# Two-layer diffusion trunk on one core: context and latent tokens packed to 1152 columns, with a padded tile for the convolutions alone

## The chip, the core and the metric

The kernel runs as one program on one core of a Trainium2 chip. The core has five engines with queues of their own: TensorE (PE; its weight loads are shown as PEld), VectorE (DVE), ScalarE (ACT), GpSimd (POOL) and SyncE (SP). Here SP issues the loads and POOL the stores. The metric is the time of one execution on the device in microseconds; lower is better. Before the change it is 2097.41 us, the median of three runs (2095.89 to 2098.44).

## What is computed

Two layers run over 128 context tokens and 1024 latent tokens with the same weights, D = 1024. Layer 0 has a Mamba-2 part (SSD) and a Hyena part (a long convolution by FFT); layer 1 is neighbourhood attention. Cut to what the change touches:

```
for l in range(2):
    h = rms_norm(x, norm_w[l]) * (1 + scale) + shift          # context and latent have their own scale, shift, gate
    if l == 0:
        z_a, xbc, dt_raw, u_b, g_b = split(h @ w_in)
        xbc = silu(depthwise_conv(xbc, conv_a_w, conv_a_b))   # 3 taps along the tokens, zeros beyond both ends
        y_a = rms_norm(ssd(xbc, dt_raw) * silu(z_a), norm_a_w)
        x0, x1, v = split(depthwise_conv(u_b, conv_b_w, conv_b_b))
        y_b = x0 * fft_long_conv(v * x1, k, hy_bias) * silu(g_b)
        out = concat([y_a, y_b]) @ w_out
    else:
        q, k, v, g = split(h @ w_in)
        out = (attention(q, k, v) * silu(g)) @ w_out
    x = x + gate * out
y = rms_norm(x, final_norm_w)
```

Context and latent are separate sequences: each convolution sees zeros before the first and behind the last token of each. The final SSD states and the context's keys and values are outputs too.

## The kernel before

Activations lie channel by channel: a tile holds 128 channels on the partitions and all tokens in its columns. Context and latent tokens share a tile. The context stands in columns 0 to 127, the latent in 130 to 1153 (`OFF` = 130); columns 128, 129 and 1154 to 1157 hold zeros, so the tile has `T` = 1158 columns, three blocks of `NB` = 386. The zeros are what a three-tap convolution needs between the two sequences and behind the last; every other step carries them along.

**Projections.** `proj` multiplies 128 output channels by all tokens. For each of three blocks it goes over the eight (in the output projection four) tiles of 128 input channels with three matmuls each, the high part of the weights by the high part of the activation (L157), high by low (L158) and low by high (L159), into one PSUM buffer of the tag `pj`, which has three. Then `evac` empties the buffer. `proj_k` with `proj_step` (L184 to L186) does the same with the loop over input channels outside, for the first chunks of a stage, whose input is still being made; `dt_proj` (L615, L616) is a small projection for dt. The values (L1167 to L1169) use 256 columns and the last projection (L1366 to L1368) 512, outside of this blocking.

**The norm.** `rstd_rep` makes 1/rms of each token, repeated over the partitions: the sum of squares comes from PE in `bg`, DVE scales it to `ms` (L326), POOL raises it to a power, `rs` (L328), DVE spreads it on a diagonal (`diag`, L334), PE multiplies that by ones (L337), and ACT copies it out (L341 to L345), with the context and the latent apart in the first third. DVE clears the pads (L330, L331). `make_h` then makes the tiles `hh` and `hl` (high and low part of h) on DVE and ACT (L359 to L365), and POOL casts the pads into each of the 16 tiles (L368, L369).

**Convolutions.** `conv_chunk` runs 36 times: for 12 chunks of xbc and 24 of u_b. It empties each block with two ACT instructions, `raw` (L586) and `acc` (L587: scaled by the middle tap, with the bias), and then adds the two outer taps on DVE in two passes over 1157 columns (L596, L598). `raw` has one buffer, `acc` three. Where the result goes to token order, `to_tokens` transposes it in slices of 128, which `tk` finds.

**Other users of the layout.** `silu2` makes z and the gates block by block (L849 on ACT, L850 on DVE). `x0g_main` loads the FFT's result `ycd`, multiplies it by the convolved x0 (L873) and by the gate with a factor 0.5 (L876). `y_tile` loads the SSD's y in two pieces around the pads and clears the pads. The output projection adds x in its part 2 (L1100, two pieces) and clears pads of x1 in part 0 (L1103, POOL). The FFT's result `yc` (tag X, one buffer) and attention's `og` have their pads cleared by DVE.

**Order.** Each engine runs its instructions in the order in which the Python code issues them. The generators of background work (SSD, FFT, the filter) are advanced by `tick` between the blocks of a projection, so that their small matmuls (`bg`) lie between the large ones; how many steps a tick takes is set by hand. POOL's queue mixes the stores with the few instructions that POOL computes, in the same order of issue, and a store waits in the queue until its tile is written.

Of the kernel before, what the change touches and what calls it, by code (L numbers as in the profile page):

```python
# [9 lines left out]
AF = mybir.ActivationFunctionType  # L10
# [6 lines left out]
OFF = 130  # L17
T = 1158
NB = 386
NCH = 9  # L20
# [16 lines left out]
def tk(c):  # L37
    return 0 if c == 0 else OFF + 128 * (c - 1)

# [5 lines left out]
class Net:  # L45
# [267 lines left out]
    def rstd_rep(self, acc, pool, ncnt, tag="tt", fill=(), p=None):  # L313

        fill = list(fill)
        nc = self.nc
        if p is None:  # L320
# [5 lines left out]
        nc.vector.tensor_scalar(out=ms, in0=p[:, :NCH], scalar1=1.0 / ncnt, scalar2=EPS, op0=ALU.mult, op1=ALU.add)  # L326
        r = self.t(pool, [128, NCH], "rs", bufs=1)
        nc.gpsimd.tensor_tensor(out=r, in0=ms, in1=self.mh, op=ALU.pow)  # L328
        rep = self.t(pool, [128, T], tag, bufs=1)
        nc.vector.memset(rep[:, 128:OFF], 0.0)  # L330
        nc.vector.memset(rep[:, OFF + 1024:T], 0.0)  # L331
        for g in range(3):
            dg = self.t(pool, [128, 3, 128], "diag", bufs=self.nd)
            nc.vector.tensor_tensor(out=dg, in0=bc(self.ident.unsqueeze(1), [128, 3, 128]),  # L334
                                    in1=bc(r[:, 3 * g:3 * g + 3].unsqueeze(2), [128, 3, 128]), op=ALU.mult)
            q = self.ps()
            nc.tensor.matmul(q[:, :384], self.ones, dg.rearrange("p a b -> p (a b)"), start=True, stop=True)  # L337
            if fill:
                fill[g - 3]()
            if g == 0:  # L340
                nc.scalar.copy(rep[:, 0:128], q[:, 0:128])  # L341
# [11 lines left out]
    def make_h(self, l, k, x, rep, slot):  # L353
# [13 lines left out]
        for sl in (slice(128, OFF), slice(OFF + 1024, T)):  # L367
            nc.gpsimd.tensor_copy(hi[:, sl], rep[:, sl])  # L368
            nc.gpsimd.tensor_copy(lo[:, sl], rep[:, sl])  # L369
# [208 lines left out]
    def conv_chunk(self, cols, pool, ps=None):  # L578

        nc = self.nc  # L580
        raw = self.t(pool, [128, T], "raw")
        acc = self.t(pool, [128, T], "acc", bufs=3)
        self.raw = raw

        def evac(b, sl, p):
            nc.scalar.copy(raw[:, sl], p)  # L586
            nc.scalar.activation(acc[:, sl], p, AF.Identity, bias=cols[:, 3:4], scale=cols[:, 1:2])  # L587
# [8 lines left out]
        V.scalar_tensor_tensor(out=acc[:, 1:T], in0=raw[:, 0:T - 1], scalar=cols[:, 0:1], in1=acc[:, 1:T],  # L596
                               op0=ALU.mult, op1=ALU.add)
        V.scalar_tensor_tensor(out=acc[:, 0:T - 1], in0=raw[:, 1:T], scalar=cols[:, 2:3], in1=acc[:, 0:T - 1],  # L598
# [72 lines left out]
    def to_tokens(self, src, dst, pool, tag, bufs):  # L671

        nc = self.nc
        o = self.t(pool, [128, T], tag, bufs=bufs)[:, 0:NCH * 128].rearrange("p (c n) -> p c n", n=128)

        def run():
            for c0 in range(0, NCH, 4):
                n = min(4, NCH - c0)
                p = self.ps()
                for j in range(n):  # L680
                    nc.tensor.transpose(p[:, j * 128:(j + 1) * 128], src[:, tk(c0 + j):tk(c0 + j) + 128], self.ident)
                nc.scalar.copy(o[:, c0:c0 + n], p[:, :n * 128].rearrange("p (a c) -> p a c", c=128))
# [4 lines left out]
    def xbc(self, pool):  # L687
# [7 lines left out]
        for j in range(12):  # L695
# [25 lines left out]
    def fft(self, g, u, pool):  # L721
# [63 lines left out]
        V.memset(yc[:, 128:OFF], 0.0)  # L785
        V.memset(yc[:, OFF + 1024:T], 0.0)
# [77 lines left out]
    def x0g_main(self, pool, second):  # L864
        nc = self.nc
        cv = self.pv[:, PV["cvb"]:PV["cvb"] + 96].rearrange("p (m j) -> p m j", j=4)
        for g in range(8):
# [3 lines left out]
            yc = self.t(pool, [128, T], "acc", bufs=3)  # L871
            self.dma(yc, self.ycd[g])
            nc.vector.tensor_tensor(out=yc, in0=yc, in1=x0, op=ALU.mult)  # L873
# [196 lines left out]
    def out0(self, part, ys, x1, pool, tail=None, mid=None, order=range(4)):  # L1070
# [24 lines left out]
        for m in range(8):  # L1095
            if part == 2:
                xr = self.t(pool, [128, T], "yr")
                self.dma(xr, self.i["xT"][:, m])
                for st, s in self.STR:
                    nc.vector.tensor_tensor(out=x1[m][:, st], in0=x1[m][:, st], in1=xr[:, st], op=ALU.add)  # L1100
            if part == 0:
                for sl in (slice(128, OFF), slice(OFF + 1024, T)):
                    nc.gpsimd.memset(x1[m][:, sl], 0.0)  # L1103
# [149 lines left out]
    def attn(self, j, qt, kt, vc, pool):  # L1253
# [17 lines left out]
        V.memset(og[:, 128:OFF], 0.0)  # L1271
        V.memset(og[:, OFF + 1024:T], 0.0)
# [583 lines left out]
```

## Time and profile before

| | us |
|---|---|
| median of 3 runs | 2097.41 |
| profiled execution | 2094.29 |
| its span | 2092.5 |
| PE busy | 2033.5 |
| DVE busy | 1316.1 |
| ACT busy | 908.5 |
| POOL busy | 122.8 |

The profile shows one execution. Its groups of instructions give line, engine, operation, tile written <- tiles read, shape and count, then busy time and the mean duration of one in ns, then the idle time of the engine just ahead of them with what ended most of it. Neighbouring matmuls overlap, so the mean duration of one is longer than their distance from each other. Of a window, the profile tells for each engine the busy time in it and the number of instructions. By the trace, the stages follow each other as the start and h (to about 60 us), xbc (to 210), z (to 500), Hyena's x1 and v with the FFT (to 850), x0 and its gate (to 1085), the output projection (to 1330), the norm ahead of layer 1 (to 1375), q, k, values, gates and attention (to 1980), and the end.

### The profile page before, as it was taken

The page shows a single profiled execution, that of the slowest core. Times are in us where ns is not written, and L with a number is a line of the kernel's source. Part 1 is how long each engine was busy: PE and PEld are TensorE (multiplying, and loading weights), DVE is VectorE, ACT ScalarE, POOL GpSimd, SP SyncE. Part 2 cuts the span into 40 slices and gives each one's busy share as a digit, 9 for nine tenths or more (in the row PEclk, how much of TensorE's full clock was granted, in tenths as well). Part 3 has the DMA queues.
Part 4 walks back from the last instruction along what each step waited for, and adds up shares of the span by engine and source line. Part 5 has one row for each costly group of instructions (what it writes and reads, how often), then busy time and mean ns, then how long its engine had stood idle before and what let it go on. Part 6 is the DMA issues. An engine that isn't in the chain of part 4 may idle for free.

```text
span 2092.5 us, 33870 instructions
## 1 busy us (share of the span) xinstructions
PE 2033.5 (97%) x13088; PEld 1836.8 (88%) x13088; DVE 1316.1 (63%) x2774; ACT 908.5 (43%) x2031; POOL 122.8 (6%) x241
## 2 busy tenths in 40 slices
PE   5999999999999999999999999999999999999998
PEld 3999997889999999888888899898888888888877
DVE  6888744145778787998889774644444344453464
ACT  4766643153333322644466512535445454443231
POOL 1110001110000000000000000200000000000000
PEclk9999999999999999999999999999999999999999
DMA  9142358554212113433353441332332223333462
GB/s 347 37 164 77 106 185 289 188 188 156 85 65 79 57 58 101 167 115 134 111 166 107 139 156 50 112 86 82 97 110 85 83 73 96 110 116 121 118 223 81
DMA packets 115417, 257.36 MB, mean 123 GB/s; under 512 B 27159, under 2 KB 63639, under 8 KB 112791
## 3 DMA queue, kind: packets, MB, share of 16 engines
q1 hardware_dynamic: 99880, 192.01, 28.9%
q0 software_dynamic: 15376, 63.18, 8.3%
q8 instruction: 104, 1.70, 0.3%
q14 instruction: 57, 0.47, 0.1%
HBM read 187.25 MB, written 67.89 MB: 122 GB/s over the span
## 4 chain that ended last, share of the span: by engine, by line
PE 51%; issue 5%; DVE 4%; DMA 2%; ACT 1%; POOL 0%; POOLq 0%; SPq 0%; DVEq 0%; ACTq 0%
PE pj L157 9%; PE pj L158 8%; PE pj L159 8%; PE bg L1329 3%; PE bg L1341 3%; PE bg L1312 3%; PE pj L1167 2%; PE pj L1168 2%; PE pj L1169 2%; PE pj L1366 1%; PE pj L1367 1%; PE pj L1368 1%; PE bg L993 1%; PE bg L1027 1%; PE bg L1006 1%
## 5 line engine op out<-in xcount | busy, mean ns | idle before, releaser
L157 PE MATMUL pj<-hh,whi 128*128 128x386 f32 x1728 | 605.0, 350 | 2.0 <-DVE gs L850 1.2
L158 PE MATMUL pj<-hl,whi 128*128 128x386 f32 x1728 | 592.2, 343 | 0.0
L159 PE MATMUL pj<-hh,wlo 128*128 128x386 f32 x1728 | 590.5, 342 | 0.0
L157 PEld LDWEIGHTS pj<-hh,whi 128*128 128x128 f32 x1728 | 327.4, 189 | 22.8 <-issue 17.9
L158 PEld LDWEIGHTS pj<-hl,whi 128*128 128x128 f32 x1728 | 326.9, 189 | 7.4 <-issue 6.3
L159 PEld LDWEIGHTS pj<-hh,wlo 128*128 128x128 f32 x1728 | 327.5, 190 | 5.4 <-issue 4.5
L130 DVE TENSOR_TENSOR wlo<-wraw,whi 128x1024 fp32r<-128x1024 f32 x108 | 131.8, 1221 | 161.7 <-ACT whi L129 154.3
L129 ACT CAST whi<-wraw 128x1024 fp32r<-128x1024 f32 x108 | 113.2, 1049 | 261.5 <-PE pj L158 227.2
L1245 DVE CUSTOM_DVE_ANT_0 sz<-bg,Tb 128x512 f32<-128x512 f32 x128 | 83.5, 687 | 128.6 <-PE bg L1312 128.0
L586 ACT COPY raw<-pj 128x386 f32<-128x386 f32 x105 | 50.4, 482 | 165.2 <-PE pj L159 76.0
L1247 ACT ACTIVATE sz<-sz,mx 128x512 f32<-128x512 f32 x128 | 91.5, 716 | 55.1 <-DVE mx L1245 54.9
L158 PE MATMUL pj<-ylo,whi 128*128 128x386 f32 x324 | 111.7, 345 | 0.0
L157 PE MATMUL pj<-yhi,whi 128*128 128x386 f32 x324 | 110.0, 340 | 0.2 <-DVE x L1084 0.2
L159 PE MATMUL pj<-yhi,wlo 128*128 128x386 f32 x324 | 109.7, 339 | 0.0
L1343 ACT COPY Pt<-bg 128x512 f32<-128x512 f32 (+1 forms) x144 | 71.9, 549 | 32.2 <-PE bg L1341 28.3
L1167 PE MATMUL pj<-whi,hh 128*128 128x256 f32 x288 | 83.5, 291 | 0.0
L1168 PE MATMUL pj<-wlo,hh 128*128 128x256 f32 x288 | 81.9, 285 | 0.0
L1169 PE MATMUL pj<-whi,hl 128*128 128x256 f32 x288 | 81.3, 283 | 0.0
L1341 PE MATMUL bg<-csq,sz 128*128 128x128 f32 x528 | 73.8, 280 | 0.0
L911 ACT ACTIVATE xw<-xt,wd 128x64 f32<-128x64 f32 x256 | 64.6, 336 | 8.2 <-PE bg L918 8.1
L1341 PEld LDWEIGHTS bg<-csq,sz 128*128 128x128 f32 x528 | 56.6, 140 | 13.0 <-issue 12.8
L1084 DVE SCALAR_TENSOR_TENSOR x<-pj,mod,x 128x128 f32<-128x128 f32 (+1 forms) x96 | 46.4, 512 | 29.1 <-PE pj L159 24.8
(427 smaller groups left out, 4041.2 us busy)
## 6 DMA issues: line engine op xcount, KB each, us to landing
wraw<-in_we SPq DMA_DIRECT2D x52, 512.0 KB, 3.7
wa<-in_wada SPq DMA_DIRECT2D x32, 512.0 KB, 6.9
wraw<-in_wo SPq DMA_DIRECT2D x24, 512.0 KB, 3.8
Tb<-Cd SPq DMA_DIRECT2D x256, 48.0 KB, 2.0
Hd<-H POOLq DMA_DIRECT2D x8, 1280.0 KB, 5.7
H<-Hd SPq DMA_DIRECT2D x8, 1280.0 KB, 6.7
xt<-xtd SPq DMA_DIRECT2D x17, 512.0 KB, 4.3
wraw<-in_woe SPq DMA_DIRECT2D x16, 512.0 KB, 3.6
```

Of the source, the lines that this page charges most:

```text
L129: self.nc.scalar.copy(hi, r)
L130: self.nc.vector.tensor_tensor(out=lo, in0=r, in1=hi.bitcast(F32), op=ALU.subtract)
L157: nc.tensor.matmul(p[:, :NB], wh, xh[k][:, sl], start=(k == 0), stop=False)
L158: nc.tensor.matmul(p[:, :NB], wh, xl[k][:, sl], start=False, stop=False)
L159: nc.tensor.matmul(p[:, :NB], wl, xh[k][:, sl], start=False, stop=(k == nk - 1))
L1167: nc.tensor.matmul(p[:, :256], self.hh[k][:, ts], hi[:, q:q + 256], start=(k == 0), stop=False)
L1168: nc.tensor.matmul(p[:, :256], self.hh[k][:, ts], lo[:, q:q + 256], start=False, stop=False)
L1169: nc.tensor.matmul(p[:, :256], self.hl[k][:, ts], hi[:, q:q + 256], start=False, stop=(k == 7))
L1245: V.tensor_tensor_reduce(out=z[:, :n], in0=s, in1=tb, scale=-1.0, scalar=3.0e38, op0=ALU.add, op1=ALU.min, accum_out=m1)
L1247: nc.scalar.activation(z[:, :n], z[:, :n], AF.Exp, bias=m1, scale=-1.0, accum_out=sm)
L1341: nc.tensor.transpose(pt[:, b * 128:(b + 1) * 128], p[:, b * 128:(b + 1) * 128], self.ident)
L1343: nc.scalar.copy(t[:, :nb * 128], pt[:, :nb * 128])
```

## The change

The latent tokens now follow the context's directly: `OFF` = 128, `T` = 1152, `NB` = 384. Only `conv_chunk` keeps a padded layout, with `PO` = 130 as the latent's first column and `TP` = 1154 columns. In it the first block (128 context and 256 latent columns) is emptied in two pieces, on each side of columns 128 and 129, which POOL clears in `raw` and `acc` of every chunk. The pads and their clearing go from every other tile. In `x0g_main` the product with x0 becomes two pieces with the factor 0.5, since its one operand is padded and the other not, and the product with the gate becomes one without the factor.

```
-OFF = 130
-T = 1158
-NB = 386
+OFF = 128
+T = 1152
+NB = 384
+
+PO = 130
+TP = 1154
...
-        nc.vector.memset(rep[:, 128:OFF], 0.0)
-        nc.vector.memset(rep[:, OFF + 1024:T], 0.0)
...
-            if g == 0:
-                nc.scalar.copy(rep[:, 0:128], q[:, 0:128])
-                nc.scalar.copy(rep[:, OFF:OFF + 256], q[:, 128:384])
-            else:
-                o = tk(3 * g)
-                nc.scalar.copy(rep[:, o:o + 384], q[:, :384])
+            nc.scalar.copy(rep[:, 384 * g:384 * g + 384], q[:, :384])
...
-        for sl in (slice(128, OFF), slice(OFF + 1024, T)):
-            nc.gpsimd.tensor_copy(hi[:, sl], rep[:, sl])
-            nc.gpsimd.tensor_copy(lo[:, sl], rep[:, sl])
...
-        raw = self.t(pool, [128, T], "raw")
-        acc = self.t(pool, [128, T], "acc", bufs=3)
+        raw = self.t(pool, [128, TP], "raw")
+        acc = self.t(pool, [128, TP], "acc", bufs=3)
         self.raw = raw
+        for t in (raw, acc):
+            nc.gpsimd.memset(t[:, 128:PO], 0.0)
 
         def evac(b, sl, p):
-            nc.scalar.copy(raw[:, sl], p)
-            nc.scalar.activation(acc[:, sl], p, AF.Identity, bias=cols[:, 3:4], scale=cols[:, 1:2])
+            for lo, hi, o in ((0, 128, 0), (128, NB, PO - OFF)) if b == 0 else ((0, NB, PO - OFF),):
+                d = slice(sl.start + lo + o, sl.start + hi + o)
+                nc.scalar.copy(raw[:, d], p[:, lo:hi])
+                nc.scalar.activation(acc[:, d], p[:, lo:hi], AF.Identity, bias=cols[:, 3:4], scale=cols[:, 1:2])
...
-            nc.vector.tensor_tensor(out=yc, in0=yc, in1=x0, op=ALU.mult)
-            gs = self.t(pool, [128, T], "acc", bufs=3)
+            nc.vector.scalar_tensor_tensor(out=yc[:, 0:128], in0=yc[:, 0:128], scalar=0.5, in1=x0[:, 0:128], op0=ALU.mult, op1=ALU.mult)
+            nc.vector.scalar_tensor_tensor(out=yc[:, OFF:], in0=yc[:, OFF:], scalar=0.5, in1=x0[:, PO:], op0=ALU.mult, op1=ALU.mult)
+            gs = self.t(pool, [128, TP], "acc", bufs=3)
             self.silu2(gs, pool)
-            nc.vector.scalar_tensor_tensor(out=yc, in0=yc, scalar=0.5, in1=gs, op0=ALU.mult, op1=ALU.mult)
+            nc.vector.tensor_tensor(out=yc, in0=yc, in1=gs[:, 0:T], op=ALU.mult)
...
-            nc.vector.memset(r[:, 128:OFF], 0.0)
-            nc.vector.memset(r[:, OFF + 1024:T], 0.0)
-            self.dma(r[:, 0:128], src[:, 0:128])
-            self.dma(r[:, OFF:OFF + 1024], src[:, OFF:OFF + 1024])
...
-                for st, s in self.STR:
-                    nc.vector.tensor_tensor(out=x1[m][:, st], in0=x1[m][:, st], in1=xr[:, st], op=ALU.add)
-            if part == 0:
-                for sl in (slice(128, OFF), slice(OFF + 1024, T)):
-                    nc.gpsimd.memset(x1[m][:, sl], 0.0)
+                nc.vector.tensor_tensor(out=x1[m], in0=x1[m], in1=xr, op=ALU.add)
...
-        V.memset(og[:, 128:OFF], 0.0)
-        V.memset(og[:, OFF + 1024:T], 0.0)
```

Left out are the same two memsets for `yc`, the offsets passed to `tk` in `to_tokens`, and slices that start at `PO` instead of `OFF` where a convolution's result is read. The lines of `conv_chunk`'s evacuation become L583 and L584, the DVE passes L593 and L595, the store L89, the power L331.

What stands in the engines' queues changes at three places. First POOL, at the norm ahead of layer 1; `rs` is the power, `ms` its input, `tt` the repeated 1/rms of which the pads are cast, `x1k` a tile whose store follows. Before, the last rows ahead of the power and the first behind it:

```order
L368 CAST hh_1863_12612<-tt_12461 128x4
L369 CAST hl_1864_12613<-tt_12461 128x4
L368 CAST hh_1866_12625<-tt_12461 128x4
L369 CAST hl_1867_12626<-tt_12461 128x4
L328 TENSOR_TENSOR rs_12459<-ms_12457,mh_76 128x9
L86 DMA x1d_93<-x1k_12362 128x9x128
```

And after, at the same place:

```order
L89 DMA out_state<-sb_10920 128x1024
L331 TENSOR_TENSOR rs_11266<-ms_11264,mh_76 128x9
L331 TENSOR_TENSOR rs_12509<-ms_12507,mh_76 128x9
L89 DMA x1d_93<-x1k_12412 128x9x128
L89 DMA x1d_93<-x1k_12439 128x9x128
```

Thirty-two casts stood between the power of the SSD's norm (`rs_11181` before, `rs_11266` after) and that of layer 1, and none does now.

Second ACT, in Hyena's stage, where a convolution's chunk is emptied (`raw`, `acc`, from the PSUM tile `pj`; `pv` holds the taps). Before:

```order
L586 COPY raw_5589<-pj_5591 128x386
L587 ACTIVATE acc_5590<-pj_5591,pv_74 128x386
L586 COPY raw_5589<-pj_5667 128x386
L587 ACTIVATE acc_5590<-pj_5667,pv_74 128x386
L129 CAST whi_5798<-wraw_5622 128x1024
```

And after:

```order
L583 COPY raw_5626<-pj_5630 128x128
L584 ACTIVATE acc_5627<-pj_5630,pv_74 128x128
L583 COPY raw_5626<-pj_5630 128x256
L584 ACTIVATE acc_5627<-pj_5630,pv_74 128x256
L583 COPY raw_5626<-pj_5708 128x384
L584 ACTIVATE acc_5627<-pj_5708,pv_74 128x384
```

Block 0 (`pj_5630`) takes four instructions where it took two; the other blocks take two as before.

Third POOL, in the same stage: `ycd` is the store of the FFT's result `X`. Before, the stores stand alone:

```order
L86 DMA sbd_89<-S_642_4130 128x1024
L86 DMA zd_88<-acc_4432 128x8x128
L86 DMA sbd_89<-S_642_4130 128x1024
L86 DMA ycd_90<-X_5046 128x1158
L86 DMA ycd_90<-X_5450 128x1158
```

After, the memsets of the chunks stand between them:

```order
L578 MEMSET acc_5451 128x2
L89 DMA ycd_90<-X_5075 128x1152
L578 MEMSET raw_5281 128x2
L578 MEMSET raw_5450 128x2
L578 MEMSET acc_5627 128x2
L89 DMA ycd_90<-X_5489 128x1152
L578 MEMSET acc_5811 128x2
L578 MEMSET raw_5626 128x2
```

So a memset for a chunk waits in the queue behind a store, and a store behind a memset. On DVE, the rows that write `X_5489` stand some 50 rows ahead of the pass that reads `raw_5626` and `acc_5627`.

More of the change, by code (lines that the diff above doesn't have):

```diff
@@ L34, with tk @@
 NPV = _o
-def tk(c):
-    return 0 if c == 0 else OFF + 128 * (c - 1)
+def tk(c, off=OFF):
+    return 0 if c == 0 else off + 128 * (c - 1)
 def bc(ap, shape):
@@ L595, in conv_chunk @@
         V = nc.vector
-        V.scalar_tensor_tensor(out=acc[:, 1:T], in0=raw[:, 0:T - 1], scalar=cols[:, 0:1], in1=acc[:, 1:T],
+        V.scalar_tensor_tensor(out=acc[:, 1:TP], in0=raw[:, 0:TP - 1], scalar=cols[:, 0:1], in1=acc[:, 1:TP],
                                op0=ALU.mult, op1=ALU.add)
-        V.scalar_tensor_tensor(out=acc[:, 0:T - 1], in0=raw[:, 1:T], scalar=cols[:, 2:3], in1=acc[:, 0:T - 1],
+        V.scalar_tensor_tensor(out=acc[:, 0:TP - 1], in0=raw[:, 1:TP], scalar=cols[:, 2:3], in1=acc[:, 0:TP - 1],
                                op0=ALU.mult, op1=ALU.add)
@@ L673, in to_tokens @@
         nc = self.nc
-        o = self.t(pool, [128, T], tag, bufs=bufs)[:, 0:NCH * 128].rearrange("p (c n) -> p c n", n=128)
+        off = OFF + src.shape[1] - T
+        o = self.t(pool, [128, src.shape[1]], tag, bufs=bufs)[:, 0:NCH * 128].rearrange("p (c n) -> p c n", n=128)
         def run():
@@ L703, in xbc @@
                 self.store(self.bctd[1:, :, j, :].rearrange("c p t -> p c t"),
-                           xs[:, OFF:OFF + 1024].rearrange("p (c t) -> p c t", t=128))
+                           xs[:, PO:PO + 1024].rearrange("p (c t) -> p c t", t=128))
                 if j < 2:
@@ L732, in fft @@
             for j in range(n):
-                c0 = OFF + (4 * b + j) * 128 if b < 2 else 0
+                c0 = PO + (4 * b + j) * 128 if b < 2 else 0
                 nc.tensor.transpose(p[:, j * 128:(j + 1) * 128], u[:, c0:c0 + 128], self.ident)
@@ L784, in fft @@
         yc = self.t(pool, [128, T], "X", bufs=1)
-        V.memset(yc[:, 128:OFF], 0.0)
-        V.memset(yc[:, OFF + 1024:T], 0.0)
         p = self.ps()
@@ L844, in silu2 @@
         nc = self.nc
-        raw = self.t(pool, [128, T], tag)
+        raw = self.t(pool, [128, dst.shape[1]], tag)
         def evac(b, sl, p):
@@ L857, in z_main @@
                 dt()
-            z = self.t(pool, [128, T], "acc", bufs=3)
+            z = self.t(pool, [128, TP], "acc", bufs=3)
             self.silu2(z, pool)
@@ L870, in x0g_main @@
             x0 = self.conv_chunk(cv[:, g], pool)
-            yc = self.t(pool, [128, T], "acc", bufs=3)
+            yc = self.t(pool, [128, TP], "acc", bufs=3)[:, 0:T]
             self.dma(yc, self.ycd[g])
-            nc.vector.tensor_tensor(out=yc, in0=yc, in1=x0, op=ALU.mult)
-            gs = self.t(pool, [128, T], "acc", bufs=3)
+            nc.vector.scalar_tensor_tensor(out=yc[:, 0:128], in0=yc[:, 0:128], scalar=0.5, in1=x0[:, 0:128], op0=ALU.mult, op1=ALU.mult)
+            nc.vector.scalar_tensor_tensor(out=yc[:, OFF:], in0=yc[:, OFF:], scalar=0.5, in1=x0[:, PO:], op0=ALU.mult, op1=ALU.mult)
+            gs = self.t(pool, [128, TP], "acc", bufs=3)
             self.silu2(gs, pool)
-            nc.vector.scalar_tensor_tensor(out=yc, in0=yc, scalar=0.5, in1=gs, op0=ALU.mult, op1=ALU.mult)
+            nc.vector.tensor_tensor(out=yc, in0=yc, in1=gs[:, 0:T], op=ALU.mult)
             if g == 6:
@@ L1048, in y_tile @@
             r = self.t(pool, [128, T], "yr")
-            if norm is None:
-                self.dma(r, src)
+            self.dma(r, src)
         if norm is not None:
-            nc.vector.memset(r[:, 128:OFF], 0.0)
-            nc.vector.memset(r[:, OFF + 1024:T], 0.0)
-            self.dma(r[:, 0:128], src[:, 0:128])
-            self.dma(r[:, OFF:OFF + 1024], src[:, OFF:OFF + 1024])
             nw = self.pv[:, PV["naw"] + k:PV["naw"] + k + 1]
```

2 lines of the change are left out of this document (1 added, 1 removed).

## The prediction

> **What bounds the kernel now.** I read the page's head first, then the windows, the groups by shape, the waits, and the timeline of the one place where the change takes something out of a chain.
>
> ```profile
> span 2092.5 us, 33870 instructions
> PE 2033.5 (97%) x13088; PEld 1836.8 (88%) x13088; DVE 1316.1 (63%) x2774; ACT 908.5 (43%) x2031; POOL 122.8 (6%) x241
> PEclk9999999999999999999999999999999999999999
> PE 51%; issue 5%; DVE 4%; DMA 2%; ACT 1%; POOL 0%; POOLq 0%; SPq 0%; DVEq 0%; ACTq 0%
> ```
>
> TensorE (PE) is busy for 2033.5 of 2092.5 us at a granted clock that stays at the top; of the chain that ended last, the largest share by far is PE's. The other engines have room. So the kernel's time is the number of matmuls times their pace, plus some 59 us in which PE stands. The waits of PE show that little of this belongs to the code the change touches:
>
> ```profile
> PE pj L184 <- ACT hh L364: 2.9, 2, 2.4
> PE bg L337 <- DVE diag L334: 2.6, 2, 1.9
> PE pj L157 <- ACT acc L587: 0.3, 1, 0.3
> ```
>
> In the whole run the projections (L157) waited once, for 0.3 us, for ACT to empty a PSUM block of a convolution. The two other rows belong to the norm in front of layer 1, below.
>
> **Part 1: two columns fewer in each matmul.** The blocks shrink from 386 to 384 columns. These rows give the number of such matmuls:
>
> ```profile
> L157 PE MATMUL pj<-hh,whi 128*128 128x386 f32 x1728 | 605.0, 350 | 2.0 <-DVE gs L850 1.2 <-DVE acc L850 0.5 <-ACT acc L587 0.3
> L159 PE MATMUL pj<-hh,wlo 128*128 128x386 f32 x1728 | 590.5, 342 | 0.0
> L158 PE MATMUL pj<-ylo,whi 128*128 128x386 f32 x324 | 111.7, 345 | 0.0
> L159 PE MATMUL pj<-yhi,wlo 128*128 128x386 f32 x324 | 109.7, 339 | 0.0
> L185 PE MATMUL pj<-hl,whi 128*128 128x386 f32 x48 | 17.2, 358 | 1.3 <-DVE hl L365 0.6 <-POOL hl L369 0.6
> L616 PE MATMUL pj<-hl,wdts 128*64 128x386 f32 x24 | 8.1, 338 | 0.0
> ```
>
> Lines 157, 158 and 159 have 1728 each on h and 324 each on y: 6156. The same three products run block by block at L184 to L186 (468), and L615/L616 make 48. Together 6672. The mean of one (350 ns) is no pace, since neighbours overlap; the pace is a window's length over its count, in stretches where PE never stands:
>
> ```profile
> 464.00:501.00 37.00, 37.00 (x211) 37.00 (x211) 16.34 (x16) 10.74 (x18) 1.99 (x3) 1.00 0.60 228
> 1234.00:1283.00 49.00, 49.00 (x281) 49.00 (x281) 22.67 (x40) 4.20 (x4) 0.00 (x0) 1.00 0.20 67
> 1383.00:1405.00 22.00, 22.00 (x188) 22.00 (x187) 0.65 (x3) 4.63 (x13) 1.31 (x2) 1.00 0.23 61
> 2015.00:2079.00 64.00, 64.00 (x277) 51.85 (x277) 37.54 (x79) 17.10 (x40) 5.13 (x8) 1.00 0.36 124
> ```
>
> The columns are: window, its length, then busy time and count of PE, weight loads, DVE, ACT and POOL, granted clock, DMA share, GB/s. The first two windows hold 386-column matmuls: 37.00/211 = 175.4 ns and 49.00/281 = 174.4 ns. The third holds the 256-column ones of the values: 22.00/188 = 117.0 ns. The fourth holds the 512-column ones of the last layer: 64.00/277 = 231.0 ns. From 256 to 512 columns the slope is 114.0/256 = 0.445 ns a column.
>
> No 384-column matmul runs in numbers, so I bound its pace from both sides. Along the slope two columns are 0.89 ns, times 6672 = **5.9 us**. The straight line from 256 to 512, on the other hand, has 174.0 ns at 384 columns, and the first window stands 1.4 ns above that: 9.3 us. The second window stands only 0.4 ns above it (2.7 us). One matmul more or less in a window is already 0.8 ns, so the rows can't settle it. I take the middle of the first two, **-7.6 us**, since the first window is of the shape with most matmuls; the ends 2.7 and 9.3 are kept for the range.
>
> The Trainium skill, page "TensorE: Matmul & The Clock Gate", section "Back-to-back issue gap", gives for a stream of weight-load and matmul pairs about 81 ns at 128 and 131 ns at 512 columns. By that, two columns would be 0.26 ns, and this part 1.7 us instead of 7.6. The trace disagrees: 231.0 ns at 512 columns, as the fourth window shows.
>
> **Part 2: the pads of h.** Before layer 1 the pad columns of 16 tiles are cast by POOL, 32 instructions. They stand in POOL's queue ahead of the power that every token's norm waits for:
>
> ```profile
> 1331.41 0.19 POOL L368 CAST hh<-tt 128x2 fp32r<-128x2 f32 x1 [156.57 <-DVE tt L331]
> 1332.00 0.17 DVE L326 TENSOR_SCALAR ms<-bg 128x9 f32<-128x9 f32 x1 [0.78 <-PE bg L351]
> 1332.22 3.71 PE L681 MATMUL bg<-csq,x 128*128 128x128 f32 x32 [0.26 <-DVE ms L326]
> 1335.23 0.19 POOL L369 CAST hl<-tt 128x4 fp32r<-128x4 f32 x1
> 1335.37 1.80 POOL L328 TENSOR_TENSOR rs<-ms,mh 128x9 f32<-128x9 f32 x1
> 1337.20 1.50 DVE L334 TENSOR_TENSOR diag<-csq,rs 128x384 f32<-128x384 f32 x3 [5.04 <-POOL rs L328]
> 1337.86 1.19 PE L337 MATMUL bg<-diag,csq 128*128 128x384 f32 x2 [1.93 <-DVE diag L334]
> 1347.08 0.78 PE L184 MATMUL pj<-hh,whi 128*128 128x386 f32 x3 [2.42 <-ACT hh L364]
> ```
>
> The means (ms) are ready at 1332.17, the casts hold POOL until 1335.4, and the power rs comes 3.2 us late. Without them rs ends at about 1334.0. PE has transposes (L681) until 1332.22 + 3.71 = 1335.93, so it can start the L337 matmuls 1.93 us earlier and no more; the chain behind (diag, L337, copies, h, L184) moves with it: **-1.9 us**. What is late next is ACT's hh at L184 (2.42 us), which shifts but stays. The low end is 0, if the chain behind is held by something else. The high end comes from the window right behind:
>
> ```profile
> 1348.00:1352.00 4.00, 3.92 (x14) 3.60 (x13) 4.00 (x7) 1.44 (x3) 0.00 (x0) 0.57 1.00 272
> ```
>
> There the granted clock is 0.57; 4.00 us at 0.57 lose 1.7 us against full clock. If PE's shorter pause spared that, the part would be worth 3.6 us.
>
> At the start of the program POOL's casts are late once: the L185 row above shows 0.6 us for POOL's hl, beside 0.6 us for DVE's hl of the same tile. Between 0 and -0.6; I take **-0.1**, since DVE stays the next to come. The memsets of two or four columns that vanish on DVE and POOL, and the two DMAs of y that become one, lie beside PE work: 0.
>
> **Part 3: the convolutions' first block in two pieces.** For each of 36 chunks ACT now empties block 0 in four instructions instead of two:
>
> ```profile
> L586 ACT COPY raw<-pj 128x386 f32<-128x386 f32 x105 | 50.4, 482 | 165.2 <-PE pj L159 76.0 <-DVE acc L598 71.8 <-PE bg L487 6.0
> L587 ACT ACTIVATE acc<-pj,pv 128x386 f32<-128x386 f32 x72 | 49.1, 683 | 0.0
> L341 ACT COPY tt<-bg 128x128 f32<-128x128 f32 x2 | 0.5, 263 | 2.0 <-PE bg L337 2.0
> L565 ACT COPY H<-bg 128x256 f32<-128x256 f32 x32 | 12.3, 384 | 0.0
> L364 ACT ACTIVATE hh<-sq,mod 128x128 fp32r<-128x128 f32 x12 | 4.8, 403 | 7.0 <-DVE sq L359 5.3 <-DVE hl L365 1.8
> ```
>
> Before: 482 + 683 = 1165 ns. After: copies 263 + 384, activations 403 and, between 403 at 128 and 683 at 386 columns, about 540: 1590 ns. That is +0.43 us a chunk, 15.3 us of ACT in all, which has PE's matmuls as its cover (PE waited 0.3 us for L587). The bounds are 0 and 15.3. Not all of the cover is thick: ACT's raw waited 71.8 us for the convolution on DVE, in ten stretches, because raw is one buffer. I let a quarter of these ten pass 0.43 us on: **+1.0 us**.
>
> The padded tiles also need their two columns cleared, 72 memsets on POOL, behind whatever store stands there:
>
> ```profile
> L1103 POOL MEMSET x<- 128x2 f32 x8 | 0.6, 105 | 32.4 <-PE pj L159 32.4
> L86 POOL DMA_DIRECT2D ycd<-X x8 | 4.3, 534 | 356.7 <-issue 118.5 <-DVE X L839 111.5 <-ACT raw L586 87.5
> ```
>
> The memset takes 0.105 us, a store's issue ahead of it 0.534. Only the convolution on DVE waits for it, not ACT. A memset of raw in turn waits for the convolution before, and queued behind it are the stores of ycd, which free the tile X. In the order of DVE, however, the rows that write X stand some 50 rows ahead of the convolution that reads the cleared columns, so the store has gone by then. I take 0; the other end is 36 x 0.64 = 23 us, if each chunk met a store.
>
> **Part 4: DVE's passes.** In the x0 stage one product of 1158 columns becomes two pieces, and in the output projection two adds become one:
>
> ```profile
> L873 DVE TENSOR_TENSOR acc<-acc,acc 128x1158 f32<-128x1158 f32 x8 | 10.9, 1358 | 0.0
> L1100 DVE TENSOR_TENSOR x<-x,yr 128x1024 f32<-128x1024 f32 x8 | 9.8, 1219 | 0.0
> L1100 DVE TENSOR_TENSOR x<-x,yr 128x128 f32<-128x128 f32 x8 | 2.3, 291 | 4.2 <-DMA yr<-in_xT 4.1
> ```
>
> Pieces cost 1219 + 291 = 1510 ns against 1358 for the whole: +0.15 us eight times in the one, -0.15 us eight times in the other. DVE is 63% busy and PE's rows name it for little; I take 0, with ends at ±1.2 us.
>
> **The sum.** -7.6 - 1.9 - 0.1 + 1.0 = -8.6 us on the profiled execution of 2094.29 us gives 2085.7 us. The median of the runs is 2097.41, 3.1 us above that execution, and a change of PE's pace acts on both alike: **2088.8 us**. A measurement of this kernel can tell about 0.2% from no change, that is 4.2 us.
>
> **Rivals.**
> (a) PE takes its columns four at a time, so 386 cost as much as 388. Then each matmul gives back 4 x 0.445 = 1.78 ns, 11.9 us in all: 2097.4 - 11.9 - 1.0 = 2084.5. For it: the first window stands 1.4 ns above the line, and a 388-column matmul would stand 0.9 above it from two columns alone. Against it: the second stands 0.4 above. The Trainium skill, page "SBUF — State Buffer", section "Door 1: The DMA port swizzle (why `[64,N]` ≈ `[32,N]`)", says SBUF is read in lines of 16 bytes, four fp32, and that each change of line is paid. It doesn't say that PE's streaming pays by whole lines, and no row here shows it alone.
> (b) The pace follows where the tiles lie as much as their width. The two 386-column windows differ by 1.0 ns; packing moves every tile, and 1.0 ns against us on 6672 matmuls is 6.7 us: 2088.8 + 6.7 = 2095.5, no measurable change. For it speaks that difference of one shape; against it that one miscounted matmul explains 0.8 ns of it.
> (c) The weight loads set the pace and columns nothing. Then only parts 2 and 3 remain: 2097.4 - 1.0 = 2096.4. Against it: 256-column matmuls run at 117.0 ns with a load each (187 loads to 188 matmuls in the third window).
> (d) The pause before layer 1 stays as it is, since another link holds it: 2088.8 + 1.9 = 2090.7.
> (e) Slower: the convolutions' chain through the single raw buffer. ACT's four pieces (0.43) and a memset behind a store (0.64) make raw free 1.07 us later in a chunk; ACT's existing waits for L598 grow by it, the three PSUM buffers fill, and PE stands. All 36 chunks would cost 38.5 us. The gain outside is 9.6 us, so it decides from nine chunks on, and is slower by over 0.2% from 13. With half of them, 18: 2097.4 - 9.6 + 19.3 = 2107.1. For it: ten stretches where ACT already waits for DVE. Against it: with 71.8 us of such waits PE lost 0.3.
>
> **How the numbers follow.** Forecast 0.50, (a) 0.18, (b) 0.14, (c) 0.04, (d) 0.07, (e) 0.07. Faster by over 0.2% (below 2093.2) are the forecast, (a) and (d): 0.75. Within it (b) and (c): 0.18. Slower 0.07. The range goes from 2081 (4 us under (a): 1.7 for the clock, and a lucky part of the tiles' places) to 2096, which leaves out (e), (c) and a part of (b), together under 0.2.
>
> **What would show it.** In the profile after, windows of the same stretches should give 174 to 174.6 ns for 384 columns; 173.6 or less speaks for (a), 175 or more for (b) or (c). rs should start within 0.1 us of ms in the norm before layer 1, and the L337 row should lose its 1.9 us wait; if it doesn't, (d). The wait of L157 for L584 (ACT's acc) should stay under 2 us; tens of us there, or under DVE's convolution, are (e). The prediction is wrong in its ground if PE's busy time doesn't fall by 5 to 10 us.

## The result, and the profile after

The changed kernel takes 2079.57 us (median of four runs, 2079.07 to 2080.80) against 2096.65 before (four runs, 2093.69 to 2098.44): a ratio of 0.9924, with a 95% interval from 0.9913 to 0.9936. Beside the experiments it was timed twice more: 0.9931 (0.9914 to 0.9948) and 0.9932 (0.9918 to 0.9946). By the medians it saves 13 to 17 us where 8.6 were forecast, and the first median lies 1.4 us under the range. Two single executions stand apart and enter no figure below: e1's profiled one, at a granted clock of 0.56, and one of e9's, of 3973.58 us.

The head of the page after, with the same lines as before:

```profile
span 2077.3 us, 33946 instructions
PE 2019.4 (97%) x13088; PEld 1820.7 (88%) x13088; DVE 1313.7 (63%) x2720; ACT 917.9 (44%) x2100; POOL 110.5 (5%) x233
PEclk9999999999999999999999999999999999999999
PE 82%; DVE 7%; DMA 4%; ACT 3%; issue 3%; SPq 0%; POOL 0%; POOLq 0%; DVEq 0%; ACTq 0%
```

The span fell by 15.2 us, and 14.1 of them are PE's busy time (2033.5 to 2019.4) at an equal number of instructions. So nearly all of the gain is a shorter distance between matmuls (below: pace), not less waiting. The same two stretches show it: 213 matmuls of the z stage and 540 of the output projection, with nothing else on PE between them. Their windows before (window, its length, then busy time and count of PE, weight loads, DVE, ACT, POOL, granted clock, DMA share, GB/s; the count is one or two high, since it takes in the matmuls at the edges):

```profile
463.64:501.34 37.70, 37.70 (x215) 37.66 (x214) 16.34 (x16) 10.74 (x18) 1.99 (x3) 1.00 0.60 227
1233.21:1328.29 95.08, 95.08 (x541) 94.86 (x542) 52.49 (x94) 19.13 (x30) 0.00 (x0) 1.00 0.17 53
```

And after, with the 512-column matmuls of the end as a third:

```profile
462.86:500.06 37.20, 37.20 (x214) 37.17 (x214) 16.23 (x16) 11.52 (x24) 2.50 (x9) 1.00 0.62 232
1231.40:1325.20 93.80, 93.80 (x540) 93.60 (x541) 51.18 (x90) 19.14 (x30) 0.00 (x0) 1.00 0.14 49
1998.27:2064.53 66.26, 66.26 (x285) 53.11 (x284) 38.22 (x80) 17.08 (x40) 5.12 (x8) 1.00 0.36 125
```

37.70/213 = 177.0 ns became 37.20/213 = 174.6, and 95.08/540 = 176.1 became 93.80/540 = 173.7. That is 2.4 ns for two columns, not 0.9. A window is one sample, so below I use the mean pace by stage, worked out from the trace: for each projection matmul the start of PE's next matmul less its own start, and of these the mean of those between 100 and 200 ns (some 6230 of 6672; the others stand beside a wait or a matmul of another kind). In ns:

| kernel | h, layer 0 | y, output projection | h, layer 1 | all | 256 columns (values) | 512 columns (end) |
|---|---|---|---|---|---|---|
| before | 176.8 | 176.0 | 176.6 | 176.60 | 118.0 | 231.9 |
| after | 175.2 | 173.5 | 173.3 | 174.40 | 115.1 | 233.3 |
| e7: before, 384 of 386 columns | 175.5 | 175.5 | 175.4 | 175.52 | 118.0 | 231.9 |
| e2: after, rows of 1158 | 175.3 | 174.7 | 174.7 | 175.05 | 118.2 | 232.4 |
| e3: after, blocks of 386 | 175.9 | 177.0 | 176.2 | | 115.4 | 233.3 |
| e10: after, h moved | 173.5 | 173.5 | 173.3 | 173.44 | 116.3 | 233.4 |
| e12: after, h moved otherwise | 175.2 | 173.5 | 173.3 | 174.41 | 115.6 | 233.3 |
| e9: after, weights and h moved | 175.2 | 173.9 | 174.7 | 174.81 | 118.0 | 228.9 |

(e7's and e3's stage columns give the 384-column and the 386-column matmuls; the other third of e3's blocks, 384 wide, ran at 174.8, 173.5 and 173.3.) Two kinds of matmul that the change did not touch moved as well: the values' 256 columns went from 118.0 to 115.1 ns, and the last 512 from 231.9 to 233.3. Width can't do that.

The norm ahead of layer 1, in the timeline after:

```profile
1328.92 0.17 DVE L329 TENSOR_SCALAR ms<-bg 128x9 f32<-128x9 f32 x1 [0.92 <-PE bg L347]
1329.15 5.38 PE L679 MATMUL bg<-csq,x 128*128 128x128 f32 x32 [0.26 <-DVE ms L329]
1329.31 1.79 POOL L331 TENSOR_TENSOR rs<-ms,mh 128x9 f32<-128x9 f32 x1 [160.38 <-ACT x1k L680]
1331.14 1.50 DVE L335 TENSOR_TENSOR diag<-csq,rs 128x384 f32<-128x384 f32 x3 [2.05 <-POOL rs L331]
1334.36 0.81 PE L338 MATMUL bg<-diag,csq 128*128 128x384 f32 x2
1341.74 0.79 PE L187 MATMUL pj<-hh,whi 128*128 128x384 f32 x3 [2.32 <-ACT hh L360]
```

The power rs starts 0.39 us after the start of ms instead of 3.4, PE waits for diag no more there, and the first matmul on h comes 12.8 us after ms where it came after 15.1 (1332.00 to 1347.08): 2.3 us.

The evacuation in pieces, by its groups and by what PE waited for:

```profile
L584 ACT ACTIVATE acc<-pj,pv 128x256 f32<-128x256 f32 x24 | 14.1, 588 | 0.0
L583 ACT COPY raw<-pj 128x256 f32<-128x256 f32 x35 | 13.2, 378 | 0.0
L584 ACT ACTIVATE acc<-pj,pv 128x128 f32<-128x128 f32 x24 | 11.2, 467 | 0.0
L583 ACT COPY raw<-pj 128x128 f32<-128x128 f32 x35 | 9.4, 268 | 107.5 <-DVE acc L595 71.2 <-PE pj L162 20.3 <-DVE acc L846 6.3
L578 POOL MEMSET raw<- 128x2 f32 x36 | 3.6, 101 | 311.8 <-DVE acc L595 193.0 <-DVE acc L698 59.4 <-DVE acc L846 50.2
```

```profile
PE pj L160 <- ACT acc L584: 0.6, 1, 0.6
```

268 + 378 + 467 + 588 = 1701 ns against 1165 before: 0.54 us a chunk, 19 us of ACT. PE's wait for these instructions is 0.6 us, against 0.3 before. POOL's memsets wait long for DVE, and DVE never for them.

### The profile page after: what moved, and what is told of

The parts are those of the page before. It is cut to its first block, busy times and chain, and to the rows that moved or that the text cites. A ratio compares the mean times of both kernels' runs of the same rounds, so it can differ in the third digit from the quotient of the medians.

```text
span 2077.3 us, 33946 instructions
## 1 busy us (share of the span) xinstructions
PE 2019.4 (97%) x13088; PEld 1820.7 (88%) x13088; DVE 1313.7 (63%) x2720; ACT 917.9 (44%) x2100; POOL 110.5 (5%) x233
## 4 chain that ended last, share of the span: by engine, by line
PE 82%; DVE 7%; DMA 4%; ACT 3%; issue 3%; SPq 0%; POOL 0%; POOLq 0%; DVEq 0%; ACTq 0%
PE pj L160 15%; PE pj L161 15%; PE pj L162 15%; PE bg L1315 3%; PE bg L1327 3%; PE bg L1298 3%; PE pj L1155 2%; PE pj L1156 2%; PE pj L1157 2%; PE bg L778 1%; PE bg L777 1%; PE bg L915 1%; PE pj L1353 1%; PE bg L290 1%; PE pj L1354 1%
## 5 line engine op out<-in xcount | busy, mean ns | idle before, releaser
L160 PE MATMUL pj<-hh,whi 128*128 128x384 f32 x1728 | 601.1, 348 | 2.7 <-DVE acc L846 1.8
L161 PE MATMUL pj<-hl,whi 128*128 128x384 f32 x1728 | 586.4, 339 | 0.0
L162 PE MATMUL pj<-hh,wlo 128*128 128x384 f32 x1728 | 586.1, 340 | 0.0
L160 PEld LDWEIGHTS pj<-hh,whi 128*128 128x128 f32 x1728 | 324.7, 188 | 23.7 <-issue 18.0
L132 ACT CAST whi<-wraw 128x1024 fp32r<-128x1024 f32 x108 | 113.3, 1050 | 259.1 <-PE pj L161 229.6
L583 ACT COPY raw<-pj 128x384 f32<-128x384 f32 (+2 forms) x140 | 56.0, 402 | 171.2 <-PE pj L162 84.0
L160 PE MATMUL pj<-yhi,whi 128*128 128x384 f32 x324 | 111.4, 344 | 3.8 <-DVE x L1076 2.8
L162 PE MATMUL pj<-yhi,wlo 128*128 128x384 f32 x324 | 110.8, 342 | 0.0
L161 PE MATMUL pj<-ylo,whi 128*128 128x384 f32 x324 | 109.7, 339 | 0.0
L160 PEld LDWEIGHTS pj<-yhi,whi 128*128 128x128 f32 x324 | 61.4, 189 | 7.1 <-issue 5.5
```

Source lines behind the costliest of these rows:

```text
L132: self.nc.scalar.copy(hi, r)
L160: nc.tensor.matmul(p[:, :NB], wh, xh[k][:, sl], start=(k == 0), stop=False)
L161: nc.tensor.matmul(p[:, :NB], wh, xl[k][:, sl], start=False, stop=False)
L162: nc.tensor.matmul(p[:, :NB], wl, xh[k][:, sl], start=False, stop=(k == nk - 1))
```

## The experiments

**Width or place?** e1, e2, e3 and e7 ask which part of the 2.2 ns comes from two columns fewer, and which from where the tiles lie. A tile's place here is the address of its first byte within a partition, modulo 512. Rows of 1152 fp32 are 4608 bytes, nine times 512, so all tiles of a pool now begin at one place, where rows of 4632 bytes spread them over many.

e1 and e7 are one kernel: the one before, its tiles left alone, with all but the first of each block's products cut to `NW` = 384 columns (`sw` begins where `sl` does). One of the lines, with the same edit in `proj_step`:

```
-                nc.tensor.matmul(p[:, :NB], wh, xl[k][:, sl], start=False, stop=False)
+                nc.tensor.matmul(p[:, :NW], wh, xl[k][:, sw], start=False, stop=False)
...
```

> The kernel before, its tiles, block starts (386 apart) and 1158-column rows kept, but of each block's 24 products all except the first one read and write only 384 columns (left out: 23 of 24 products of the last two columns of each block). Theory width (fewer columns alone give the gain): the matmuls' pace falls from 176.6 ns to about 174.3 ns as in the changed kernel, 14 to 15 us less than before. Rival place (only two columns' worth comes from width, the rest from where the tiles lie): about 175.7 ns, 6 us less than before.

> e1's kernel again (the kernel before with 384 of 386 columns multiplied, 23 of 24 products of two columns a block left out), since the clock of e1's profile was 0.56 and its pace can't be read; e1's times were 0.997 of the kernel before. Width alone at the slope of 0.445 ns a column: pace 175.7 ns, 6 us under the kernel before. If a width that is a multiple of 64 bytes gives more by itself, at block starts that aren't: 174.3 ns, 14 us under.

e1 took 0.9972 of the kernel before (0.9960 to 0.9985), e7 0.9963 (0.9950 to 0.9976): 6.5 and 7.5 us by the medians. e7's pace is 175.52 ns, 1.08 under before, and the two stretches stand between before and after:

```profile
465.12:502.55 37.43, 37.43 (x214) 37.39 (x214) 16.35 (x16) 10.76 (x18) 1.99 (x3) 1.00 0.61 229
1232.67:1327.55 94.88, 94.88 (x541) 94.70 (x542) 52.54 (x94) 19.13 (x30) 0.00 (x0) 1.00 0.17 55
```

So width alone is 1.08 x 6672 = 7.2 us, close to the 7.6 of the prediction, and half of the gain in pace.

e2 keeps the changed kernel's width and spreads its tiles again (the same for the low part, and for both parts of y):

```
-        hi = self.t(self.p_h, [128, T], f"hh{k}", F32R)
+        hi = self.t(self.p_h, [128, 1158], f"hh{k}", F32R)[:, 0:T]
...
```

> The changed kernel, its 384-column blocks and everything else kept, but each of the high and low tiles that the projections read is laid out 1158 columns apart as before, so their first bytes fall on all places of a 512-byte row instead of on one or two. Theory width: pace 174.3 ns and the time of the changed kernel, 2079.6 us. Rival place: 175.7 ns, 9 us more than the changed kernel (about 2089).

2083.06 us, 0.9958 (0.9946 to 0.9971), by the ratios 5 to 7 us more than the changed kernel. Its pace is 175.05 ns, 0.65 above the changed kernel's, and the values are back at 118.2. In the long stretch:

```profile
1232.63:1326.93 94.30, 94.30 (x540) 94.11 (x541) 51.13 (x90) 19.11 (x30) 0.00 (x0) 1.00 0.15 50
```

From 95.08 (before) over 94.88 (width) and 94.30 (block starts at multiples of 384 as well) to 93.80 (tiles at one place): the place is a cause of its own. e2 differs from e7 in the rest of the change too, so that the step between these two belongs to the block starts is argued, not shown. The rival was right, with about half of the size expected.

e3 keeps the place and widens two blocks of three:

> The changed kernel, tiles and block starts kept, but the first two of each three blocks are multiplied 386 columns wide (two columns of the next block, thrown away). Theory width at 1.1 ns a column: the mean pace goes from 174.3 to 175.9 ns, 10 us more than the changed kernel. Two columns at the slope of 0.445 ns: 0.6 ns more in the mean, 4 us more. If an even pace depends on a width of 384 as well as on the place, the two blocks go back to 176.6 ns: 10 us more, and the third block stays.

2085.88 us, 0.9974 (0.9958 to 0.9990), by the ratios 9 to 10 us over the changed kernel. The 386-column blocks ran at 177.0 ns on y, where the 384-column ones beside them kept 173.5, and at 176.2 on layer 1's h against 173.3: 2.9 to 3.5 ns for two columns (in layer 0, 1.1). The third reading holds: the even pace of 173.3 to 173.5 ns needs the width too. Neither the slope (0.9 ns) nor columns counted in fours (1.8 ns) gives that.

**Which place?** In the changed kernel the program puts the weights of the projections at 160, layer 0's h at 352 and layer 1's at 480. e4 puts an unused tile ahead of layer 0's h:

```
+        self.t(hst.enter_context(self.pool("pad")), [128, 32], "pad")
         self.p_h = hst.enter_context(self.pool("h"))
```

> The changed kernel with 128 unused bytes ahead of layer 0's sixteen tiles of h, so that they begin at 480 instead of 352 within 512 bytes, as layer 1's do. In the trace of the changed kernel layer 0's matmuls on h run at 175.1 ns and all later ones at 173.3. If the place within 512 bytes sets this, layer 0 falls to 173.3 too: 1.75 ns on 3792 matmuls, 6.6 us less than the changed kernel (about 2073). If it is the stage (work of other engines beside it), nothing changes: 2079.6.

Layer 0's pace fell from 175.2 to 173.5 ns: the place, not the stage. The time was 2076.77 us (0.9930, 0.9911 to 0.9950), which I could not tell from the changed kernel's. The next runs paired it on one chip.

> The changed kernel itself, as the yardstick for the three others on the same chip. Pace of layer 0's matmuls on h 175.2 ns, of all later ones 173.4, and 0.992 of the time of the kernel before.

> Layer 0's tiles of h moved by 128 bytes, as in e4, beside the changed kernel on the same chip. e4's trace showed layer 0's pace at 173.5 ns instead of 175.2 (1.7 ns on 3792 matmuls, 6.4 us), while its time stood only some 3 us under the changed kernel's of another call. If the pace carries through: 6 us under e5. If something else takes its place (the granted clock, a wait): 0 to 3 us under e5.

e5 took 2077.68 us (0.9931), e6 2080.10 (0.9936, 0.9919 to 0.9953): no gain in time, at a layer 0 pace of 173.5 against 175.1. In windows of 20 us, the granted clock under 1 cost 17.2 us in e6's profiled execution and 10.4 in e5's (the sum of 20 us times what was missing). The 6.8 us between them are as much as the pace gained, in these two executions. They don't explain the medians: by the mean clocks of all executions e6 lost 14.5 us and e5 12.5, and of two executions of e6 at 0.995 one took 2073.68 us and one 2080.24.

e9, e10 and e12 move h and the weights to other places, to find what the place is measured from. The distance below is the place of the streamed tile less that of the tile loaded as weights, modulo 256.

> The changed kernel with 128 unused bytes ahead of the weights' tiles, which moves the weights from 160 to 288 within 512 bytes and layer 0's h from 352 to 480; layer 1's h stays at 480. If the place of the streamed tile itself sets the pace (480 good, 352 bad): 173.4 ns in all stages. If its distance from the weights sets it (480 - 160 = 320 good, 352 - 160 = 192 bad): now all h lie 192 from the weights, and layer 0 and layer 1 both run at 175.1 ns. Time: e6 showed that 6 us of pace need not show in the time; 2076 to 2080 for the first, 2080 to 2084 for the second.

> The changed kernel with layer 0's h at 224 within 512 bytes (384 unused bytes ahead of it). 480 and 352 have the same place within 128 bytes and not within 256, where 480 and 224 agree. If the place within 256 bytes decides: 173.4 ns in layer 0. If within 512: 175 to 176 ns. Time by the pace alone 2072 or 2079, and up to 6 us more where the granted clock takes it back, as in e6.

> The changed kernel with layer 0's h at 96 within 512 bytes (256 unused bytes ahead of it), which agrees with 352 within 256 bytes. If the place within 256 bytes decides: 175.1 ns in layer 0, as in the changed kernel, and its time (2078). If within 512: another pace, between 173.3 and 177.

e10 gave 173.5 ns in layer 0, e12 175.2: places 256 bytes apart are alike. e9 gave 175.2 in layer 0 with h at 480, and layer 1's h, which had not moved, went from 173.3 to 174.7 when the weights did. The windows of the z stage, at full clock, e10 ahead of e12 (36.93/213 = 173.4 ns and 37.20/213 = 174.6):

```profile
460.26:497.19 36.93, 36.93 (x214) 36.90 (x214) 16.21 (x16) 11.53 (x24) 2.99 (x9) 1.00 0.63 234
463.20:500.40 37.20, 37.20 (x214) 37.17 (x214) 16.22 (x16) 11.52 (x24) 2.49 (x8) 1.00 0.62 231
```

Nor is it the new place of the weights: most tiles of y multiplied between 1080 and 1220 us moved along with them in e9, by the program's addresses, and kept 173.1 to 173.8 ns in windows of 20 us. Those after them stayed behind, now at a distance of 192, and went from 173.3 to 173.9 at first to 174.6 to 174.8 from 1280 us on. So at 384 columns it is the distance, within 256 bytes: 64 (after's layer 1, e4, e10) is good and 192 (after's layer 0, e9, e12) is not. No other distance was tried by itself. In the 512-column matmuls of the end the projection's weights are the streamed side, and y is loaded; there the distance went from 192 to 64, and the pace from 233.3 to 228.9:

```profile
2004.60:2069.61 65.01, 65.01 (x286) 53.33 (x284) 38.17 (x80) 17.09 (x40) 5.13 (x8) 1.00 0.38 127
```

The values, 256 columns, stream the weights too, and their distance made the same move, from 192 to 64. They became slower, 118.0 ns where the changed kernel had 115.1. A stretch of them in the changed kernel and in e9, 196 and 188 matmuls (113.3 and 117.8 ns):

```profile
1374.88:1397.09 22.21, 22.21 (x198) 22.21 (x197) 1.57 (x9) 4.74 (x13) 1.31 (x2) 1.00 0.33 88
1376.90:1399.04 22.14, 22.14 (x190) 22.14 (x189) 0.78 (x4) 4.71 (x13) 1.31 (x2) 1.00 0.23 61
```

So which distance is the good one changes with the width, and one distance can't be called good for all matmuls.

e9's time was 2084.09 us (0.9951, 0.9934 to 0.9968), e10's 2078.69 (0.9930), e12's 2079.29 (0.9934).

**The pause before layer 1.** e8 makes rs late again in the changed kernel:

```
-        nc.gpsimd.tensor_tensor(out=r, in0=ms, in1=self.mh, op=ALU.pow)
...
+            W = [128, 3, NCH]
...
+            nc.gpsimd.tensor_tensor(out=r, in0=bc(ms.unsqueeze(1), W), in1=bc(self.mh.unsqueeze(1), W), op=ALU.pow)
```

> The changed kernel, with the power ahead of layer 1 done by POOL over 27 columns (three copies of ms) instead of 9, so that rs comes late again, by about 2.6 us (the 18 further columns at 0.146 ns x 1000, from one column in 0.63 us and nine in 1.8). PE's transposes end 5.3 us after ms starts. If the casts' delay of rs was what cost PE its pause, as the prediction said: rs now ends about 4.8 us after ms, diag comes at 5.0 to 5.6, L337's matmul waits about 0.5 to 1 us, and the first matmul on h moves from 12.8 us to about 13.3 us after ms (it was 15.1 before, with rs ending at 5.2). If something else shortened the pause: it stays at 12.8.

```profile
1325.88 0.17 DVE L329 TENSOR_SCALAR ms<-bg 128x9 f32<-128x9 f32 x1 [0.92 <-PE bg L353]
1326.27 4.64 POOL L333 TENSOR_TENSOR rs<-ms,mh 128x27 f32<-128x27 f32 x1 [160.13 <-ACT x1k L686]
1331.60 0.88 PE L344 MATMUL bg<-diag,csq 128*128 128x384 f32 x2
1339.05 0.80 PE L187 MATMUL pj<-hh,whi 128*128 128x384 f32 x3 [2.33 <-ACT hh L366]
```

rs ended 5.0 us after ms, PE stood for 0.12 us ahead of L344, and the first matmul on h came 13.2 us after ms, near the 13.3 expected; 0.4 later than in the first profile of the changed kernel (12.8) and 1.8 later than in e5 on the same chip (11.4). This agrees with the prediction, by which a late rs costs PE the time by which it outlasts the 32 transposes. But here these took 5.4 us where they took 3.7 before, so that time was short, and the 15.1 us of before do not come back. What differs is the granted clock, the third number from the right in these windows of four us, of before and of e8:

```profile
1336.00:1340.00 4.00, 2.14 (x8) 1.63 (x9) 2.11 (x5) 1.45 (x5) 4.00 (x4) 0.79 0.31 125
1340.00:1344.00 4.00, 4.00 (x23) 3.13 (x22) 0.00 (x0) 3.47 (x10) 3.20 (x4) 0.78 0.98 261
```

```profile
1326.00:1330.00 4.00, 3.90 (x20) 3.90 (x21) 0.05 (x1) 2.87 (x9) 3.73 (x1) 0.57 0.30 108
1330.00:1334.00 4.00, 3.88 (x28) 3.05 (x27) 2.11 (x5) 3.86 (x10) 4.00 (x5) 1.00 0.39 112
```

Before, the clock was low behind the wait, 0.79 and 0.78 over 8 us, or 1.7 us of full clock; in e8 it was low ahead of it, 0.57 over 4 us, under the 32 transposes, which hid rs's delay. In e5 it was 1.00 from the transposes to the first matmul on h, which came at 11.4. Of the 2.3 us, then, 1.93 are the wait that is gone, and the rest, as far as these four profiles tell, goes with the moment at which the clock dips. The time of e8, 2078.51 us, can't tell 2 us.

**The first block in two pieces.** e11 empties all three blocks so, e13 none (it leaves out the zeros between the two sequences). In short:

```
e11: for lo, hi, o in ((0, 128, 0 if b == 0 else PO - OFF), (128, NB, PO - OFF)):
e13: PO = 128, TP = 1152, no memsets, evac as in the kernel before
```

> The changed kernel with all three blocks of each convolution emptied in two pieces instead of the first alone: 72 more blocks at 0.54 us (1701 ns for four instructions against 1163 for two in the changed kernel's groups), 39 us more of ACT. If PE's work covers ACT there, as the prediction's +1.0 us for the first block implies: 0 to 2 us over the changed kernel of e5, and L160's wait for L584 stays under 3 us. If the chain through the single raw buffer is exposed (the rival on the slower side): 20 to 39 us more.

> The changed kernel with the padded tile taken out of the convolutions: 1152 columns, the first block emptied in one piece, no memsets (left out: the zeros between the two sequences, so the taps at their border read the neighbour sequence). It saves 36 x 0.54 = 19 us of ACT and 72 memsets of POOL. If the cost grows evenly with ACT's work, as e11's 6 to 8 us on 39 suggest: 3 to 4 us under e14. If the prediction's term was right: 1 us under e14. If the cover held wholly for the first piece: no difference.

> The changed kernel, yardstick for e13, e15 and e16 on the same chip: 0.993 of the kernel before; layer 0's pace 175.1 ns.

e11 took 2085.42 us (0.9964, 0.9950 to 0.9977): 6 us over e12 on the same chip, which e11's expectation put at 0 to 2 or at 20 to 39. L160's wait for L584 stayed at 0.6 us there, so the cost does not come by the way of the rival; in the profiled executions the granted clock cost 2.0 us more than in e12 (14.2 and 12.2), and the rest is not settled. e13 took 2077.85 us (0.9928, 0.9913 to 0.9942) against 2079.42 for e14 (0.9932, 0.9918 to 0.9946). ACT was busy for 907.3 us instead of e14's 919.1:

```profile
PE 2018.3 (97%) x13088; PEld 1820.2 (88%) x13088; DVE 1314.2 (63%) x2720; ACT 907.3 (44%) x2028; POOL 103.6 (5%) x161
```

So the two pieces of the first block cost 1.6 us by the medians. Each interval reaches some 3 us to either side: nothing, the forecast's 1 us and the 3 to 4 that e11 suggested are all possible, the rival's 20 and more are not.

**A faster version?**

> e10 again, layer 0's h at 224: pace 173.4 ns in layer 0. If the pace carries through to the time: 6 us under e14. If the granted clock and waits take it back, as e6 suggests: 0 to 2 us under e14, with more of the span lost to a granted clock under 1 than in e14.

> e15 with the last projection's weights moved by 128 bytes too. In e9, which had this distance, the 512-column matmuls ran at 228.9 ns instead of 233.3; here it applies to 306 of them, 1.3 us. 1 us under e15 if it carries through.

e15 took 2076.28 us (0.9921, 0.9907 to 0.9935), 3.1 us under e14; e16 2077.57 (0.9926, 0.9911 to 0.9940), though its 512 columns ran at 229.9 ns. Beside the changed kernel, or e12 with its distances, on the same chip, the better place of layer 0 stands 2.4 us over (e6), 0.6 under (e10) and 3.1 under (e15); all intervals overlap, and no version here is shown to beat the changed kernel. In e15's profile the clock took as much as in e14's (10.4 and 10.6 us), and PE was busy for 2015.9 us instead of 2019.8: of the 6 us of pace only 4 arrive in the busy time. Part of the loss shows at the seams, where a projection's matmul on layer 0's h is followed by a small one of the background: the steps from the one to the other's start take 45.7 us in all instead of 43.3 (e10 45.4 against e12's 43.2). One more thing limits what the distance says: e14's z stretch, at the same places as in the first profile after, took

```profile
463.66:500.58 36.92, 36.92 (x214) 36.89 (x214) 16.23 (x16) 11.54 (x24) 2.49 (x8) 1.00 0.62 233
```

which is the even pace, 173.3 ns. At a distance of 192 a stretch can run evenly or not; over layer 0 the mean was 175.1 to 175.2 in all profiles.

## Why the prediction was wrong, point by point

- **What bounds the kernel**: right. PE is the bound, and 14.1 of 15.2 us are its busy time.
- **Part 1, the step that failed**: for the width itself it was right. Two columns fewer, alone, gave 1.08 ns and 7.2 us (e7) where -7.6 was taken. But the part took the pace as a matter of columns only. The place of the tiles was put at nothing in the sum, and left to rival (b) as a spread of 1.0 ns "against us". It was the missing term: 0.47 ns from e7 to e2 (the block starts, as argued) and 0.65 ns with the rows of 4608 bytes (e2 to after), together 1.12 x 6672 = 7.5 us, all of it gain. The values' 864 matmuls, which the prediction held fixed and even used as a yardstick, added 2.9 ns each, 2.5 us.
- The hint stood in the rows: two windows of one shape differed by 1.0 ns. I explained 0.8 of it by a miscounted matmul instead of asking what the new row length does to the places. The counts were indeed too high by the matmuls at the edges: windows cut at matmuls give 177.0 and 176.1 ns, not 175.4 and 174.4. By the table's means (118.0, 176.6 and 231.9 ns) 386 columns stood 1.65 ns above the straight line at 384, or 11 us, so that the middle would have been 8.5 instead of 7.6. That the 7.6 came so near to 7.2 is in part luck.
- **Part 2, the pads of h**: right; -1.9 forecast, 2.3 us in the trace, of which the wait is 1.93; e8 agrees with the mechanism, but put it to a small test only (0.12 us of wait).
- **Part 3, the pieces**: in keeping with the runs; +1.0 forecast, 1.6 us by e13, with some 3 us to either side, though a chunk took 0.54 us more instead of 0.43. Rival (e), the slower side, did not come: ACT waited 71.2 us for L595 in ten stretches, as before.
- **Part 4**: nothing seen of it.
- **The rivals**: (a) would have given 2084.5 and is refuted by e3 and e7, where two columns cost 2.9 to 3.5 ns in one place and 1.08 in another. The Trainium skill's lines of 16 bytes (page "SBUF — State Buffer", section "Door 1: The DMA port swizzle (why `[64,N]` ≈ `[32,N]`)") give neither. (b) was right in its cause and wrong in its sign. (c) is refuted by e7. (d) did not come: the pause became shorter. The Trainium skill's figure of about 131 ns for 512 columns (page "TensorE: Matmul & The Clock Gate", section "Back-to-back issue gap") agrees with none of these profiles (228.9 to 233.4).
- **The sum**: paces 14.7, values 2.5, pause 2.3, less 0.5 for the 512 columns: 19.0 us. The lower clock cost 9.0 us in the execution profiled after and 10.6 in the one before, which makes it 20.6, against 15.2 in the spans. Some 5 us are taken back; e15 shows such a loss at the seams, and e13 allows some for the pieces. Which it is here stays open.

## What to carry to other kernels

Where a kernel stands on TensorE's pace, a new row length changes two things: how many columns are streamed, and where every tile lies towards the weights; count both, and look at matmuls that the change doesn't touch, since they show the second alone. Rows that are a multiple of 512 bytes put all tiles of a pool at one distance, which can then be chosen, for each width by its own trace. A pace gained is not yet time: the better distance for layer 0 gained 6 us of pace and no time that these runs can tell.

## What the runs showed of the hardware that was not expected

- The pace of an fp32r matmul of 384 columns depends on the distance between streamed tile and weights within 256 bytes: 173.3 to 173.5 ns at 64, 175.2 in the mean at 192. At 512 columns it is 228.9 at 64 and 233.3 at 192. At 256 columns it is the other way: 118.0 at 64 (e9) and 115.1 to 116.4 at 192 (the runs with the changed kernel's layer 1).
- At the good distance 386 columns run at 176.2 to 177.0 ns and 384 at 173.3 to 173.5: two columns cost 2.9 to 3.5 ns. Spread over many places, they cost 1.1.
- Faster matmuls went with more time at a lower granted clock in e6's profile (17.2 us against e5's 10.4), but not in e15's (10.4 against e14's 10.6) or e10's (12.2, as e12's).
